# Loading the last two kept weight units into dead query and key buffers, and making mean and eps of the group norms on VectorE

## The chip, the cores and the metric

One Trainium2 chip; the kernel runs on one of its cores. The metric is the device time of one execution in microseconds (us), the median of the runs shown. Engines are named as in the profile: PE is TensorE (matmuls and transposes; PEld its weight loads), DVE is VectorE, ACT is ScalarE, POOL is GpSimd, SP is SyncE, which here only issues transfers. A "q" behind an engine's name means its queue of instructions.

## The reference

Two layers of an encoder on 256 tokens of width 1024, in float32. Each layer has a mixer and a channel part:

```python
def mixer_sublayer(x, n1, w_in_l, qg, kg, rpb_l, og, w_out_l, tables):
    h = rms_norm(x, n1)
    proj = h @ w_in_l                                  # 1024 -> 2560
    qa, ka, va, qd, kd, vd, qc, kc, vc = jnp.split(proj, cuts, axis=-1)
    ...                                                # q and k: norm per head, rotary for d and c
    out_a = neighbourhood_attention(qa, ka, ...)       # 4 heads
    out_d = dilated_window_attention(qd, kd, ...)      # 6 heads
    out_c = gqa_block_attention(qc, kc, ...)           # 6 heads of queries, 2 of keys
    mix = jnp.concatenate([rms_norm(out_a, og[:NA_W]), rms_norm(out_d, ...), rms_norm(out_c, ...)], axis=-1)
    return x + mix @ w_out_l                           # 1024 -> 1024

def channel_sublayer(x, n2, w_gu, cw, cb, w_dn):
    g, u = jnp.split(rms_norm(x, n2) @ w_gu, 2, axis=-1)      # 1024 -> 2 x 2816
    g = depthwise_conv_centred(g, cw, cb)                     # 3 taps along the tokens
    return x + (jax.nn.gelu(g, approximate=False) * u) @ w_dn # 2816 -> 1024
```

The three norms of `mix`, one for each group of heads, are the group norms of the title: `lax.rsqrt(mean(x*x) + EPS)` over the 256 or 384 columns of a group.

## The kernel before, in words

**Weights.** Every float32 weight is split into a high part (rounded to the format that PE multiplies, by a cast on ACT) and a low part (the rest, by a subtraction on DVE), and a product is made of three matmuls: high by high, high by low, low by high (`mm3`). The weights come in units of up to 128 x 2048 numbers, in the order of use: 12 units of the input projection, 6 of the output projection, 33 of the channel part, for each layer. `unit()` hands out the next unit; it first issues loads up to four units ahead into a ring of four buffers (`raw`, queue of SP), and splits up to two units ahead into a ring of two pairs of buffers (`hi` and `lo` in the pool `wp`). A unit's pair comes free when its last matmul is done.

**Kept units.** The 6 units of the output projection of the second layer are split early, during the channel part of the first layer (`keep`), and their parts are stored in DRAM (`dram_khi`, `dram_klo`). When such a unit is due, `split` has nothing to split: it loads both parts with two transfers from the queue of POOL into the next pair of the ring. Units 0 to 3 of the six have 128 x 1536 numbers a part (768 KB), units 4 and 5 have 128 x 1024 (512 KB). In this document "unit 0" to "unit 5" are these six.

**Mixer.** PE weaves the matmuls of the projections between the small ones of the attention (scores, transposes of the probabilities, weighing of the values). Queries and keys of one kind of head lie in tiles `act_q..` and `act_k..` as high and low part: `qo`, `ko` for the dilated and the neighbourhood heads, `qc`, `kc` for the grouped heads. The last scores that read `qc` and `kc` are those of heads 10 and 11; the neighbourhood heads come after them. `mixed` writes each pair of heads' output into `mixT` as high and low part and adds up the squares on POOL (`act_sqm`). `group_rstd` turns the squares with PE (two transposes), sums them on DVE (`small_ss`) and calls `rstd_of`: mean and eps (`small_ms`), then the power -0.5 (`small_rstd`), both on POOL. `rstd_of` also serves the norms per head, there with `width` 64. The output projection of a group runs without the norm; DVE multiplies by it when it adds the product to `xs` (`const_x`): four such updates for each group, one for each half of the tokens and of the columns.

**From the mixer to the channel part.** Units 4 and 5 are the last group's: unit 4 the left half of the columns, unit 5 the right half. When the left half of `const_x` is up to date, PE transposes it (8 transposes), ACT and DVE write it as high and low part into `act_hT`, and the first matmuls of the channel part read that.

**Order.** The kernel records every operation (`Plan.add`), and a planner (`Plan.order`) then writes them out engine by engine: of all operations that could start it takes the one that it expects to start first, by its own costs for each kind of operation, and between equal ones that with the lower rank. The rank is the place in the program plus a shift (`later`) plus a number from the table `PLACES`, which holds one for some of the operations. Every engine runs its instructions in the written order. All of them are issued on one line, so every row of the profile names L472, and rows are told apart by their tiles.

Of the kernel before, what the change touches and what calls it, by code (L numbers as in the profile page):

```python
# [12 lines left out]
F32R = mybir.dt.float32r  # L13
I32 = mybir.dt.int32
AF = mybir.ActivationFunctionType
ALU = mybir.AluOpType
AX = mybir.AxisListType

P = 128
# [4 lines left out]
HD = 64  # L24
# [12 lines left out]
UNIT = 2048  # L37
# [187 lines left out]
def handover(a, b):  # L225
# [1 line left out]


PLACES = {
# [6 lines left out]
}  # L236


class Plan:
# [5 lines left out]
    def pool(self, real, name, bufs, space=bass.MemoryType.SB):  # L245
        return PlanPool(self, real, name, bufs, space)
# [271 lines left out]
def encoder_kernel(  # L518
# [21 lines left out]
    nc = Plan(tc)  # L540
# [5 lines left out]
    act = pool("act", 2)  # L546
# [19 lines left out]
    def load_x(c, n, by):  # L566
        cs = slice(c * P, (c + n) * P)
        by.dma_start(xs[:, :, cs], xv[:, :, cs])
# [53 lines left out]
    raws, parts, taken = [], [], [0]  # L622
# [3 lines left out]
    kept = {}  # L626
# [16 lines left out]

    def load(i):
        v = views[i]
        if i in kept:
            raws.append(None)
            return
        a, b = v.shape[1], v.shape[2]
        raw = wp.tile([P, UNIT], F32, tag="raw", name=f"raw{i}", bufs=RAWS)  # L650
        rv = raw[:, : a * b].rearrange("p (a b) -> p a b", b=b)
        if i == 0:
            for by, what, c in START:
                by = nc.scalar if by == "act" else nc.sync
                if what == "w":
                    by.dma_start(rv[:, c], v[:, c])
                elif what == "x":
                    load_x(*c, by)
                elif what == "ident":
                    by.dma_start(ident, c_ident)  # L660
                elif what == "g":
                    by.dma_start(gl0 if c == 0 else gl1[16 * c - 16 : 16 * c], gsrc[c])
            nc.first_loads = len(nc.ops)
        else:
            for c in range(0, a, 2 if i == 1 else a):
                e = c + 2 if i == 1 else a
                nc.sync.dma_start(rv[:, c:e], v[:, c:e])
        raws.append(raw)

    def split(i):  # L670
        v = views[i]
        a, b = v.shape[1], v.shape[2]
        n = a * b
        raw = raws[i]
        hi = wp.tile([P, UNIT], F32R, tag="hi", name=f"hi{i}", bufs=PARTS)
        lo = wp.tile([P, UNIT], F32R, tag="lo", name=f"lo{i}", bufs=PARTS)
        h = b if i < 2 else b * max(1, CHUNK // b)
        if i in kept:
            for d, z in zip(kept[i], (hi, lo)):
                nc.gpsimd.dma_start(z[:, :n], d)  # L680
        for c in range(0, n if i not in kept else 0, h):
            e = min(c + h, n)
            nc.scalar.copy(hi[:, c:e], raw[:, c:e])
            nc.vector.tensor_tensor(lo[:, c:e], raw[:, c:e], hi[:, c:e].bitcast(F32), op=ALU.subtract)
        r = lambda z: z[:, :n].rearrange("p (a b) -> p a b", b=b)
        parts.append((r(hi), r(lo)))

    def unit():

        i = taken[0]  # L690
        taken[0] += 1
        with nc.later(SPLIT_LATER):
            while len(raws) < min(i + AHEAD + RAWS - PARTS, len(views)):
                load(len(raws))
            while len(parts) < min(i + AHEAD, len(views)):
                split(len(parts))
        return parts[i]
# [6 lines left out]
    def rstd_of(ss, n, width, eps, name):  # L704

        ms = small.tile([P, n], F32, tag="ms", name=f"ms_{name}")
        nc.gpsimd.tensor_scalar(ms, ss, 1.0 / width, eps, ALU.mult, ALU.add)
        r = small.tile([P, n], F32, tag="rstd", name=f"rstd_{name}")
        nc.gpsimd.tensor_tensor(r, ms, minus_half[:, :n], op=ALU.pow)
        return r  # L710
# [161 lines left out]
    def tables_of(l):  # L872
        for which in "qk":
            tables["d" + which, l] = tables_d(l, which)
        for which in "qk":
            tables["c" + which, l] = tables_c(l, which)

    load(0)
    for l in range(DEPTH):

        hT = act.tile([P, KD, 2, S], F32R, tag="hT", name=f"hT{l}", bufs=1)
        hT_hi, hT_lo = hT[:, :, 0], hT[:, :, 1]
        if l == 0:
            gains_T(0, 1)
            split(0)
# [656 lines left out]
```

## Time and profile before

| | |
|---|---|
| median of 3 runs | 611.07 us (609.97 to 611.33) |
| the profiled execution: its time, its span | 611.12 us, 609.3 us |
| granted TensorE clock, mean | 0.999 |
| PE busy | 600.6 us, 99% of the span |
| DVE busy | 484.9 us, 80% |
| ACT busy | 428.4 us, 70% |
| POOL busy | 84.6 us, 14% |
| moved by DMA | 121.44 MB, 199 GB/s over the span |
| instructions | 9892 |

The span runs from the first to the last instruction; the execution's time has 1.8 us more around it. Matmuls are pipelined: one that is shown with 0.39 us is followed by the next 0.23 us later, so a busy PE may still wait, and short waits are read from the distance of two starts rather than from the busy share. The layers follow each other as mixer (to about 121 us), channel part (to 305), mixer (to 420), channel part.

### The profile page before, as it was taken

The page shows a single profiled execution, that of the slowest core. Times are in us where ns is not written, and L with a number is a line of the kernel's source. Part 1 is how long each engine was busy: PE and PEld are TensorE (multiplying, and loading weights), DVE is VectorE, ACT ScalarE, POOL GpSimd, SP SyncE. Part 2 cuts the span into 40 slices and gives each one's busy share as a digit, 9 for nine tenths or more (in the row PEclk, how much of TensorE's full clock was granted, in tenths as well). Part 3 has the DMA queues.
Part 4 walks back from the last instruction along what each step waited for, and adds up shares of the span by engine and source line. Part 5 has one row for each costly group of instructions (what it writes and reads, how often), then busy time and mean ns, then how long its engine had stood idle before and what let it go on. Part 6 is the DMA issues. An engine that isn't in the chain of part 4 may idle for free.

```text
span 609.3 us, 9892 instructions
## 1 busy us (share of the span) xinstructions
PE 600.6 (99%) x3496; PEld 525.2 (86%) x3496; DVE 484.9 (80%) x989; ACT 428.4 (70%) x1065; POOL 84.6 (14%) x136
## 2 busy tenths in 40 slices
PE   8999999999999999999999999999999999999997
PEld 6999898888888888888899989887888888888886
DVE  4899987998779886978788898758977777777775
ACT  6889999686657666766598898757765556665661
POOL 2733130202400000000032214232000000000000
PEclk9999999999999999999999999999999999999999
DMA  8994223656598996999445626554666556556501
GB/s 272 296 294 143 62 79 107 208 175 240 185 219 288 318 338 220 373 311 305 142 142 189 224 70 242 184 199 139 208 207 200 169 185 208 173 176 204 198 10 69
DMA packets 85217, 121.44 MB, mean 199 GB/s; under 512 B 9880, under 2 KB 69880, under 8 KB 85168
## 3 DMA queue, kind: packets, MB, share of 16 engines
q1 hardware_dynamic: 82896, 112.17, 56.8%
q0 software_dynamic: 1728, 8.39, 4.0%
q8 instruction: 27, 0.44, 0.3%
q10 hardware_dynamic: 544, 0.26, 0.2%
q14 instruction: 22, 0.18, 0.1%
HBM read 110.93 MB, written 9.88 MB: 198 GB/s over the span
## 4 chain that ended last, share of the span: by engine, by line
PE 91%; POOL 2%; issue 2%; DMA 2%; ACT 1%; DVE 1%; SPq 0%; DVEq 0%; POOLq 0%
PE psw_w L472 50%; PE psa_a L472 41%; DMA wp_hi<-dram_khi 1%; POOL small_rstd L472 1%; DMA wp_raw<-in_w_in_dram 1%; ACT act_s2k L472 1%; POOL small_ms L472 0%; DVE const_x L472 0%; ACT act_hT L472 0%; POOL act_sck L472 0%; POOL act_scq L472 0%; ACT wp_hi L472 0%; SPq L472 0%; POOL const_gq L472 0%; POOL act_sqm L472 0%
## 5 line engine op out<-in xcount | busy, mean ns | idle before, releaser
L472 DVE TENSOR_TENSOR wp_lo<-wp_raw,wp_hi 128x512 fp32r<-128x512 f32 (+2 forms) x332 | 232.3, 734 | 55.1 <-ACT wp_hi L472 34.9
L472 ACT CAST wp_hi<-wp_raw 128x512 fp32r<-128x512 f32 (+2 forms) x332 | 202.4, 663 | 25.1 <-PE psw_w L472 9.9
L472 PE MATMUL psw_w<-act_hT,wp_hi 128*128 128x512 f32 x704 | 180.7, 393 | 0.0
L472 PEld LDWEIGHTS psw_w<-act_hT,wp_hi 128*128 128x128 f32 x704 | 127.8, 189 | 24.2
L472 PE MATMUL psa_a<-wp_hi,act_hT 128*128 128x384 f32 (+2 forms) x448 | 113.3, 333 | 2.0 <-ACT act_hT L472 1.3
L472 PEld LDWEIGHTS psw_w<-act_hT,wp_lo 128*128 128x128 f32 x704 | 98.4, 190 | 7.1
L472 PE MATMUL psw_w<-act_hT,wp_lo 128*128 128x256 f32 x704 | 103.0, 282 | 0.0
L472 PEld LDWEIGHTS psa_a<-wp_hi,act_hT 128*128 128x128 f32 x448 | 77.9, 189 | 5.0 <-ACT act_hT L472 1.6
L472 ACT COPY act_s2k<-psw_w 128x256 f32<-128x256 f32 x88 | 32.4, 373 | 61.7 <-PE psw_w L472 61.4
L472 PE MATMUL psa_a<-wp_lo,act_hT 128*128 128x384 f32 (+2 forms) x224 | 74.0, 332 | 0.1
L472 PE MATMUL psa_a<-wp_hi,act_cl 128*128 128x512 f32 (+1 forms) x176 | 68.8, 393 | 0.0
L472 PE MATMUL psa_a<-wp_lo,act_ch 128*128 128x512 f32 (+1 forms) x176 | 68.7, 392 | 0.0
L472 PE MATMUL psa_a<-wp_hi,act_ch 128*128 128x512 f32 (+1 forms) x176 | 68.3, 392 | 0.0
L472 DVE TENSOR_TENSOR act_s2k<-psw_w,act_s2k 128x256 f32<-128x256 f32 x88 | 36.6, 421 | 16.2 <-ACT act_s2k L472 15.9
L472 PEld LDWEIGHTS psa_a<-wp_lo,act_hT 128*128 128x128 f32 x224 | 42.2, 188 | 2.1 <-DVE wp_lo L472 1.0
L472 PEld LDWEIGHTS psa_a<-wp_hi,act_cl 128*128 128x128 f32 x176 | 33.1, 188 | 7.4
L472 PEld LDWEIGHTS psa_a<-wp_hi,act_ch 128*128 128x128 f32 x176 | 33.2, 189 | 6.7
L472 PEld LDWEIGHTS psa_a<-wp_lo,act_ch 128*128 128x128 f32 x176 | 33.1, 188 | 6.8
L472 DVE SCALAR_TENSOR_TENSOR act_s2k<-act_s2k,act_cw,act_s2k 128x255 f32<-128x255 f32 x88 | 36.8, 477 | 1.4 <-ACT act_s2k L472 1.3
L472 ACT ACTIVATE act_s2k<-act_s2k 128x512 f32<-128x512 f32 x22 | 13.9, 632 | 29.6 <-DVE act_s2k L472 29.6
L472 ACT ACTIVATE act_s2k<-act_s2k,act_cw 128x256 f32<-128x256 f32 x44 | 24.1, 595 | 15.0 <-DVE act_s2k L472 15.0
L472 POOL TENSOR_TENSOR small_rstd<-small_ms,const_mh 128x6 f32<-128x6 f32 (+2 forms) x26 | 31.3, 1204 | 2.1
(120 smaller groups left out, 795.2 us busy)
## 6 DMA issues: line engine op xcount, KB each, us to landing
wp_raw<-in_w_gate_up_dram SPq DMA_DIRECT2D x44, 1024.0 KB, 5.2
wp_raw<-in_w_down_dram SPq DMA_DIRECT2D x22, 1024.0 KB, 4.9
wp_raw<-in_w_in_dram SPq DMA_DIRECT2D x14, 768.0 KB, 4.7
wp_raw<-in_w_in_dram SPq DMA_DIRECT2D x8, 1024.0 KB, 8.9
wp_raw<-in_w_out_dram SPq DMA_DIRECT2D x8, 768.0 KB, 10.0
dram_khi<-act_mixT_hi SPq DMA_DIRECT2D x4, 768.0 KB, 4.4
dram_klo<-act_mixT_lo SPq DMA_DIRECT2D x4, 768.0 KB, 11.2
wp_lo<-dram_klo POOLq DMA_DIRECT2D x4, 768.0 KB, 4.7
```

What stands on the lines that cost most here:

```text
L472: getattr(o.engine.real, o.method)(*map(real, o.args), **{k: real(v) for k, v in o.kw.items()})
```

## The change

Three things are changed.

1. Units 4 and 5 of the kept ones (those whose two parts fit where one full unit would, `2 * n <= UNIT`) no longer go through the ring. Their four loads are issued by `load`, so up to two units earlier in the program, into the buffers of `kc` (unit 4) and `qc` (unit 5), which are dead once the scores of the grouped heads are done; the buffers grow from 768 to 1024 columns. `split` only passes the tiles on. The first channel units therefore follow units 2 and 3 in the ring.
2. `rstd_of` makes mean and eps on DVE where `width` is over 64, that is for the six group norms. The power stays on POOL.
3. `PLACES` has other numbers, so the planner writes another order.

```diff
 PLACES = {
-    539: 34, 543: 38, 665: 15, 834: 24, 881: 160, 919: 134, 926: 7, 974: -38, 1092: 342, 1180: -15, 1181: -15,
...
+    375: -35, 488: 15, 528: -53, 550: 173, 587: -78, 594: 125, 616: -286, 646: -9, 709: -79, 750: -226, 752: -396,
...
     def load(i):
         v = views[i]
+        a, b = v.shape[1], v.shape[2]
+        n = a * b
         if i in kept:
             raws.append(None)
+            if 2 * n <= UNIT:
+                zs = [act.tile([P, n], F32R, tag=f"{'qk'[i % 2]}c{j}", name=f"kept{i}{j}", bufs=1) for j in range(2)]
+                for z, d in zip(zs, kept[i]):
+                    nc.gpsimd.dma_start(z, d)
+                raws[-1] = [z.rearrange("p (a b) -> p a b", b=b) for z in zs]
             return
-        a, b = v.shape[1], v.shape[2]
...
     def split(i):
...
         raw = raws[i]
+        if isinstance(raw, list):
+            parts.append(raw)
+            return
...
     def rstd_of(ss, n, width, eps, name):

         ms = small.tile([P, n], F32, tag="ms", name=f"ms_{name}")
-        nc.gpsimd.tensor_scalar(ms, ss, 1.0 / width, eps, ALU.mult, ALU.add)
+        by = nc.vector if width > HD else nc.gpsimd
+        by.tensor_scalar(ms, ss, 1.0 / width, eps, ALU.mult, ALU.add)
```

POOL, second half of the mixer of layer 2, before. `dram_khi` and `dram_klo` are the kept parts, `wp_hi_240` with `wp_lo_248` is one pair of the ring and `wp_hi_141` with `wp_lo_149` the other; 1536 columns mark units 2 and 3 here, 1024 columns unit 4:

```order
L472 TENSOR_SCALAR small_ms_454<-small_ss_4031 128x2
L472 TENSOR_TENSOR small_rstd_460<-small_ms_454,const_mh_85 128x2
L472 DMA wp_lo_248<-dram_klo_2446 128x1536
L472 TENSOR_TENSOR act_sqm_866<-act_sqm_866,act_sqm_967 128x256
L472 DMA wp_hi_240<-dram_khi_2431 128x1536
L472 DMA wp_lo_149<-dram_klo_2618 128x1536
L472 DMA wp_hi_141<-dram_khi_2583 128x1536
L472 TENSOR_TENSOR act_sqm_866<-act_sqm_866,act_sqm_967 128x256
L472 TENSOR_SCALAR small_ms_300<-small_ss_1189 128x2
L472 TENSOR_TENSOR small_rstd_328<-small_ms_300,const_mh_85 128x2
L472 DMA wp_hi_240<-dram_khi_2730 128x1024
L472 DMA wp_lo_248<-dram_klo_2759 128x1024
```

The same place now, from the loads of unit 1:

```order
L472 DMA wp_lo_149<-dram_klo_2309 128x1536
L472 DMA wp_hi_141<-dram_khi_2281 128x1536
L472 DMA act_kc_965<-dram_klo_2742 128x1024
L472 TENSOR_TENSOR small_rstd_460<-small_ms_454,const_mh_85 128x2
L472 DMA act_kc_959<-dram_khi_2725 128x1024
L472 DMA act_qc_809<-dram_khi_2846 128x1024
L472 DMA act_qc_818<-dram_klo_2860 128x1024
L472 TENSOR_TENSOR act_sqm_881<-act_sqm_881,act_sqm_950 128x256
L472 DMA wp_hi_240<-dram_khi_2443 128x1536
L472 DMA wp_lo_248<-dram_klo_2478 128x1536
L472 DMA wp_lo_149<-dram_klo_2619 128x1536
L472 DMA wp_hi_141<-dram_khi_2589 128x1536
```

The four loads of units 4 and 5 moved from the end of the mixer to a place ahead of units 2 and 3, the first of them ahead of the first group's power. Of unit 2 the high part is now loaded first, with no addition of squares between its two loads; before it came second, behind such an addition. The rows of mean and eps (`small_ms`) are gone from this queue.

PE, end of the mixer of layer 2, before. `psa` are the sums of the output projection (unit 4 in 157 and 175, unit 5 in 302 and 332), the rows with `const_x` transpose its left half:

```order
L472 MATMUL psa_a_175<-wp_lo_248,act_mixT_hi_856 128x512
L472 MATMUL psa_a_175<-wp_hi_240,act_mixT_lo_916 128x512
L472 MATMUL psa_a_157<-wp_lo_248,act_mixT_hi_856 128x512
L472 MATMUL psa_a_157<-wp_hi_240,act_mixT_lo_916 128x512
L472 MATMUL psw_w_117<-const_ident_89,const_x_79 128x128 x4
L472 MATMUL psw_w_83<-const_ident_89,const_x_79 128x128 x4
L472 MATMUL psa_a_302<-wp_hi_141,act_mixT_hi_856 128x512
L472 MATMUL psa_a_302<-wp_lo_149,act_mixT_hi_856 128x512
L472 MATMUL psa_a_302<-wp_hi_141,act_mixT_lo_916 128x512
```

The same place now (unit 4 in 157 and 302, unit 5 in 332 and 175):

```order
L472 MATMUL psa_a_302<-act_kc_965,act_mixT_hi_875 128x512
L472 MATMUL psa_a_302<-act_kc_959,act_mixT_lo_920 128x512
L472 MATMUL psa_a_332<-act_qc_809,act_mixT_hi_875 128x512
L472 MATMUL psa_a_332<-act_qc_818,act_mixT_hi_875 128x512
L472 MATMUL psw_w_83<-const_ident_89,const_x_79 128x128
L472 MATMUL psw_w_117<-const_ident_89,const_x_79 128x128
L472 MATMUL psa_a_332<-act_qc_809,act_mixT_lo_920 128x512
L472 MATMUL psa_a_332<-act_qc_809,act_mixT_hi_875 128x512
L472 MATMUL psa_a_332<-act_qc_818,act_mixT_hi_875 128x512
L472 MATMUL psa_a_332<-act_qc_809,act_mixT_lo_920 128x512
L472 MATMUL psw_w_83<-const_ident_89,const_x_79 128x128 x3
L472 MATMUL psw_w_117<-const_ident_89,const_x_79 128x128 x3
```

Between the two transposes of the last group's squares and the first transpose of `const_x` stood 12 matmuls of 512 columns, all of unit 4; now 17 stand there, three of unit 3, the 12 of unit 4 and two of unit 5. Four more of unit 5 lie between the first two and the other six transposes, and six behind them, where all 12 were.

DVE at the same time, before. `small_ss` sums the squares of the last group, `small_rstd_351` is its power, `small_rstd_328` that of the second group; the rows with `const_x` are the updates, those with `wp_lo` split units of the channel part:

```order
L472 SCALAR_TENSOR_TENSOR const_x_79<-psa_a_302,small_rstd_328,const_x_79 128x512
L472 SCALAR_TENSOR_TENSOR const_x_79<-psa_a_332,small_rstd_328,const_x_79 128x512
L472 TENSOR_REDUCE small_ss_1418<-psw_w_124 128x2
L472 COPY act_cw_1498<-psw_w_166 128x88
L472 SCALAR_TENSOR_TENSOR const_x_79<-psa_a_175,small_rstd_351,const_x_79 128x512
L472 SCALAR_TENSOR_TENSOR const_x_79<-psa_a_157,small_rstd_351,const_x_79 128x512
L472 TENSOR_TENSOR wp_lo_248<-wp_raw_138,wp_hi_240 128x512 x3
```

And now:

```order
L472 TENSOR_REDUCE small_ss_1412<-psw_w_166 128x2
L472 COPY act_cw_1500<-psw_w_124 128x88
L472 TENSOR_SCALAR small_ms_344<-small_ss_1412 128x2
L472 SCALAR_TENSOR_TENSOR const_x_79<-psa_a_175,small_rstd_328,const_x_79 128x512
L472 TENSOR_TENSOR wp_lo_149<-wp_raw_95,wp_hi_141 128x512 x2
L472 SCALAR_TENSOR_TENSOR const_x_79<-psa_a_157,small_rstd_351,const_x_79 128x512
L472 TENSOR_TENSOR wp_lo_149<-wp_raw_95,wp_hi_141 128x512
L472 SCALAR_TENSOR_TENSOR const_x_79<-psa_a_302,small_rstd_351,const_x_79 128x512
```

An update of the second group went from ahead of the sum to behind it, mean and eps stand on DVE, and three splits went in between and ahead of the two updates that the transposes need.

10 rows, old and new, of the table PLACES are left out of this document.

## The prediction

> **What bounds the kernel now.** I read the page's busy times first, then the same by stage, then TensorE's timeline wherever the distance of two starts shows a wait.
>
> ```profile
> span 609.3 us, 9892 instructions
> PE 600.6 (99%) x3496; PEld 525.2 (86%) x3496; DVE 484.9 (80%) x989; ACT 428.4 (70%) x1065; POOL 84.6 (14%) x136
> 8.00:121.00 113.00, 112.12 (x747) 101.08 (x746) 100.20 (x252) 99.40 (x324) 36.35 (x55) 1.00 0.59 183
> 305.00:420.00 115.00, 113.57 (x757) 103.21 (x755) 90.84 (x239) 93.09 (x309) 31.37 (x47) 1.00 0.53 175
> 420.00:605.00 185.00, 185.00 (x990) 159.02 (x988) 139.83 (x237) 110.95 (x203) 1.26 (x3) 1.00 0.51 168
> ```
>
> A row by stage gives window, length, busy time of PE, PEld, DVE, ACT and POOL, clock, DMA share and GB/s. PE is busy 185.00 of 185 us in the last channel part, at clock 1.00, and the change takes no matmul away. So only waits of PE can be won: 0.88 us by these rows in the first mixer, 1.43 us in the second. Since pipelined matmuls cover part of a wait, the distances of starts tell more:
>
> ```profile
> 397.66 0.47 PE L472 MATMUL psa_a<-wp_hi,act_mixT_lo 128*128 128x512 f32 x1
> 398.39 0.50 PE L472 MATMUL psa_a<-wp_hi,act_mixT_hi 128*128 128x512 f32 x1 [0.26 <-DMA wp_hi<-dram_khi]
> ...
> 411.53 0.38 PE L472 MATMUL psw_w<-const_ident,act_sqm 128*128 128x128 f32 x2
> ...
> 414.18 0.40 PE L472 MATMUL psa_a<-wp_lo,act_mixT_hi 128*128 128x512 f32 x1
> 414.42 0.40 PE L472 MATMUL psa_a<-wp_hi,act_mixT_lo 128*128 128x512 f32 x1
> 415.92 1.09 PE L472 MATMUL psw_w<-const_ident,const_x 128*128 128x128 f32 x8 [1.10 <-DVE const_x L472]
> ```
>
> A 512-column matmul starts 0.24 us after the one before it (414.18 to 414.42). Against that pace PE loses 398.39 - 397.66 - 0.24 = 0.49 us on the high part of unit 2, and 415.92 - 414.42 - 0.24 = 1.26 us on `const_x` at the end of the mixer. These are the two waits that the change can reach best.
>
> **Unit 2's loads.** Before, POOL issues the low part, adds squares, then issues the high part:
>
> ```profile
> 390.19 0.60 POOL L472 DMA_DIRECT2D wp_lo<-dram_klo  x1 [5.12 <-PE psa_a L472]
> 390.81 0.75 POOL L472 TENSOR_TENSOR act_sqm<-act_sqm,act_sqm 128x256 f32<-128x256 f32 x1
> 391.50 0.57 POOL L472 DMA_DIRECT2D wp_hi<-dram_khi  x1
> wp_lo<-dram_klo POOLq DMA_DIRECT2D x1, 768.0 KB, 4.7
> wp_hi<-dram_khi POOLq DMA_DIRECT2D x1, 768.0 KB, 6.8
> ```
>
> The last two rows are the DMA view: KB and us from issue to landing. The pair lands at 390.19 + 4.7 = 394.9 and 391.50 + 6.8 = 398.3. The first matmul that needs the high part starts at 398.39, so the row's releaser is right. Now the high part goes first, from 390.2 when the buffers come free, and is there at about 394.9; the low part, wanted one matmul later, follows at about 390.8 + 6.8 = 397.6 at worst. Without the wait both are wanted at 397.9 to 398.2. The 0.49 goes; what is late next is the low part, by nothing or by 0.1.
>
> **The four early loads.** They need the end of the last scores that read `kc` and `qc`:
>
> ```profile
> 383.44 0.98 PE L472 MATMUL psw_w<-act_kc,act_qc 64*128 64x256 f32 x12
> 384.35 0.72 POOL L472 TENSOR_TENSOR small_rstd<-small_ms,const_mh 128x2 f32<-128x2 f32 x1
> 411.15 0.57 POOL L472 DMA_DIRECT2D wp_lo<-dram_klo  x1
> wp_lo<-dram_klo POOLq DMA_DIRECT2D x1, 512.0 KB, 4.0
> wp_hi<-dram_khi POOLq DMA_DIRECT2D x1, 512.0 KB, 4.7
> 371.55 0.37 SPq L472 DMA_DIRECT2D wp_raw<-in_w_down_dram  x1
> 395.84 0.32 SPq L472 DMA_DIRECT2D act_s2k<-in_conv_w_dram  x1
> L472 POOL DMA_DIRECT2D wp_hi<-dram_khi x6: 530/543/625, 371.0 to 411.7; - x6
> L472 POOL DMA_DIRECT2D wp_lo<-dram_klo x6: 530/586/787, 370.2 to 411.2; - x6
> ```
>
> The first can go at 383.44 + 0.98 = 384.4. The last two rows hold the least, median and longest issue: POOL is held 0.53 to 0.79 us by each. In the new queue the first load, the first group's power (0.72), three more loads and an addition (0.75) stand ahead of unit 2: with about 0.5 of gaps POOL gets there at 386.4 + 4h, h being the hold per load. With h = 0.55 that is 388.6, before unit 2's buffers come free at 390.2. The power comes 0.65 later; it is queued behind the first load, and DVE's updates of unit 0 wait for it, but unit 0's matmuls run until 390.2. I price that at nothing. As transfers, a pair of 512 KB lands 4.0 and 0.57 + 4.7 = 5.3 after the first issue, so 1.3 more per load, and four land at 384.4 + 4.0 + 3 x 1.3 = 392.3. SP issues nothing between 371.55 and 395.84, so they meet no other load. Unit 2's high part may be served behind them by under a microsecond (0 to 0.8 of the 3 it has from 394.9 to 397.9). Units 4 and 5 are wanted from about 412: 20 us early.
>
> **The end of the mixer.** Let T be the start of the squares' transposes (411.53). The chain to `const_x`:
>
> ```profile
> 412.82 0.41 DVE L472 TENSOR_REDUCE small_ss<-psw_w 128x2 f32<-128x256 f32 x1
> 414.45 1.41 DVE L472 SCALAR_TENSOR_TENSOR const_x<-psa_a,small_rstd,const_x 128x512 f32<-128x512 f32 x2 [1.06 <-PE psa_a L472]
> 413.33 0.19 POOL L472 TENSOR_SCALAR small_ms<-small_ss 128x2 f32<-128x2 f32 x1 [1.07 <-DVE small_ss L472]
> 413.61 0.71 POOL L472 TENSOR_TENSOR small_rstd<-small_ms,const_mh 128x2 f32<-128x2 f32 x1
> L472 DVE RECIPROCAL small_rs<-small_rs 128x2 f32<-128x2 f32 x32 | 5.1, 159 | 3.2 <-ACT act_s2k L472 3.0
> 115.22 1.28 DVE L472 TENSOR_TENSOR wp_lo<-wp_raw,wp_hi 128x512 fp32r<-128x512 f32 x2
> ```
>
> Before, the sum of squares started at T + 1.29 behind two updates, the power was done at 414.32 = T + 2.8, but the updates ran from T + 2.92, when unit 4's matmuls let them, and the transposes started at T + 4.39. PE had nothing to put between: unit 5's loads were issued with unit 4's, at 411.15 and later, and landed by 411.72 + 4.7 = 416.4.
>
> Now the sum starts near T + 0.3 and is done at T + 0.7; mean and eps on DVE are not shown by this trace, and the nearest row is the reciprocal of the same shape, 0.16 us. Behind a copy that gives T + 1.1, and the power T + 1.9. DVE's queue meanwhile has one update (0.7, from about T + 1.2 when unit 3's three matmuls are through), two splits (1.28), the first update of unit 4 (0.7), a split (0.64) and the second update. The first is done at T + 4.0, the second at T + 5.4. PE has 17 matmuls, so reaches the first transposes at T + 0.25 + 17 x 0.24 = T + 4.3, and, two transposes (0.2) and four matmuls later, the other six at T + 5.5. Both waits end before PE comes; margin 0.3 and 0.1, so I take 0.15 as left of the 1.26: gain 1.1. What is late next is `act_hT`: behind the last transpose 6 matmuls (1.4 us) cover ACT's and DVE's writing, where 12 (2.9 us) did. I keep 0 to 0.8 of loss for that in the range.
>
> **First mixer and tail.**
>
> ```profile
> 117.45 0.40 PE L472 MATMUL psa_a<-wp_hi,act_mixT_lo 128*128 128x512 f32 x1
> 117.90 0.44 PE L472 MATMUL psw_w<-const_ident,const_x 128*128 128x128 f32 x2
> 115.23 0.72 POOL L472 TENSOR_SCALAR small_ms<-small_ss 128x2 f32<-128x2 f32 x1 [2.83 <-DVE small_ss L472]
> 116.03 1.03 POOL L472 TENSOR_TENSOR small_rstd<-small_ms,const_mh 128x2 f32<-128x2 f32 x1
> 604.83 0.39 PE L472 MATMUL psa_a<-wp_hi,act_cl 128*128 128x512 f32 x1
> 605.03 0.48 DVE L472 SCALAR_TENSOR_TENSOR const_x<-psw_w,small_rx,const_x 128x256 f32<-128x256 f32 x1 [0.55 <-PE psw_w L472]
> 605.43 0.74 DVE L472 SCALAR_TENSOR_TENSOR const_x<-psa_a,small_rx,const_x 128x512 f32<-128x512 f32 x1
> ```
>
> In the first mixer mean and eps took 0.72 on POOL beside DVE's splits; on DVE, at 0.16, the chain is some 0.5 shorter, and PE's wait there, 117.90 - 117.45 - 0.24 = 0.21, mostly goes: gain 0.15, bounds 0 and 0.2. At the very end the last update starts 0.4 after the one ahead of it; in the new order that one's matmuls end some eight earlier, so the last follows its own matmul: gain 0.15, bounds 0 and 0.3. Six times mean and eps on DVE add 6 x 0.16 = 1 us to an engine at 80%, off the path elsewhere: nothing.
>
> **The sum.** 0.49 + 1.1 + 0.15 + 0.15 = 1.9, less 0.1 for the low part of unit 2. From the profiled execution's 611.12 (span 609.3 and 1.8 around it; 0.05 over the median, so no correction): 609.3 us. About 0.2%, 1.2 us, is what a measurement of this kernel can tell from no change.
>
> **Rivals.**
>
> *A. The new order brings waits of its own.* PE's order differs from before nearly from end to end. The old order has waits of 0.2 to 0.5 at places where DVE, ACT or a load comes late; four new ones of 0.4 take 1.6 of the 1.8: 610.9, no change. For it: margins of 0.1 to 0.3 above, and PE waits at few places now, so more places can get a wait than lose one. Against: the places that I followed gain. Chance 0.18. With over 3 us of such waits it would be 612.4 or more: 0.08.
>
> *B. POOL's queue holds unit 2 up (slower).* All loads share POOL's queue in order. Unit 2's high part lands 4.7 after its issue and is wanted at 396.7 to 397.9 (396.7 if PE comes there with nothing else to weave in), so PE is late once POOL arrives after 392.0: 386.4 + 4h > 392.0, h over 1.4. With 1.4 gained elsewhere, it is slower by over 1.2 once PE's wait passes 2.6: h over 2.05. If each load held POOL until it landed, 4.3 from the rows above, POOL would arrive at 403.6: a wait of 11.6, and 621. Against it: twelve issues at 0.53 to 0.79, though DVE was busy 90.84 of 115 us. Chance 0.10 in both forms, since this trace has no four loads in a row.
>
> The milder form is an issue that waits until DVE is between two pieces of work. A burst of DVE as quoted, two updates (1.41) alone or with two splits (1.28) behind them, gives h = 0.55 + 1.41 = 2.0 or 0.55 + 2.69 = 3.2, arrival at 394.4 or 399.2, a wait of PE of 2.4 or 7.2, and 611.12 - 1.4 + 2.4 = 612.1 or 616.9. I give this 0.06 and the hold until landing 0.04.
>
> The Trainium skill, "SBUF — State Buffer", says in the box on the "DVE blocks DMA" trap (section on the two sides of SBUF) that a load from GpSimd's queue cannot have its descriptors written while VectorE runs an operation that takes the port they share. It speaks against this change, which puts four such loads in a row beside VectorE's work; the twelve issues of this trace do not show such a hold.
>
> *C. The order removes more.* Other small waits may go too: the first mixer's row leaves 0.88 us idle, of which I counted 0.15. With the other 0.73 gone, and the 0.25 that I left standing: 609.3 - 1.0 = 608.3. Chance 0.04.
>
> *D. The loads are early in the program but not in time,* because they wait in order behind the last scores. The working above says 384.4 against 411.15; it would take 27 us to undo them. Under 0.02.
>
> **How the numbers follow.** The forecast holds 0.60, from 608.4 to 609.9 by the bounds of its terms; C adds 0.04 and D none. A's 0.18 lies between 609.9 and 612.3, nearly all within 1.2 of no change; A's tail (0.08) and B (0.10) are slower. So faster 0.64, same 0.17, slower 0.19. The range takes in the forecast, C and nearly all of A: 608.1 to 612.0, and leaves out B and A's tail, 0.18.
>
> **What would show it.** Right: four loads issued at 384 to 388 and landed by 393; unit 2's high part issued by 391; no `DMA wp_hi<-dram_khi` on PE; the sum of squares before T + 0.5, and under 0.3 lost at the first transposes of `const_x`; last update within 0.2 of its matmul. Wrong: loads that hold POOL over 1.4 us, PE waiting for `act_hT` at the start of the channel part, or distances over 0.35 at many other places.

## The result: 1.5 us faster

| | before | changed |
|---|---|---|
| median | 610.31 us (609.97 to 611.33, 9 runs) | 608.81 us (607.83 to 610.04, 9 runs) |
| the profiled execution: its time, its span | 611.12 us, 609.3 us | 608.41 us, 606.6 us |

The ratio is 0.9972, with a 95% interval of 0.9963 to 0.9981: 1.2 to 2.3 us less. The forecast was 609.3, 1.8 us below the first median of before (611.07, three runs); the difference measured over nine runs each is 1.5. The forecast time lies 0.5 above the measured one; the median of before itself fell by 0.8 with more runs. The two profiled executions lie 2.7 us apart, more than the medians do: that of before is 0.8 above its median, the changed one 0.4 below.

### The profile page after: what moved, and what is told of

The parts are those of the page before. It is cut to its first block, busy times and chain, and to the rows that moved or that the text cites. A ratio compares the mean times of both kernels' runs of the same rounds, so it can differ in the third digit from the quotient of the medians.

```text
span 606.6 us, 9899 instructions
## 1 busy us (share of the span) xinstructions
PE 600.9 (99%) x3496; PEld 526.7 (87%) x3496; DVE 484.9 (80%) x995; ACT 428.6 (71%) x1065; POOL 80.9 (13%) x130
## 4 chain that ended last, share of the span: by engine, by line
PE 96%; ACT 2%; DVE 1%; POOL 0%; issue 0%; DVEq 0%; ACTq 0%; POOLq 0%
PE psw_w L472 53%; PE psa_a L472 43%; ACT act_s2k L472 1%; ACT wp_hi L472 0%; DVE act_z L472 0%; DVE wp_lo L472 0%; POOL small_rstd L472 0%; ACT act_z L472 0%; ACT act_hT L472 0%; DVE act_sw L472 0%; POOL small_ms L472 0%; DVE const_x L472 0%; DVE act_qo L472 0%; POOL const_warm L472 0%; DVEq L472 0%
## 5 line engine op out<-in xcount | busy, mean ns | idle before, releaser
L472 DVE TENSOR_TENSOR wp_lo<-wp_raw,wp_hi 128x512 fp32r<-128x512 f32 (+2 forms) x332 | 231.5, 731 | 59.1 <-ACT wp_hi L472 39.3
L472 ACT CAST wp_hi<-wp_raw 128x512 fp32r<-128x512 f32 (+2 forms) x332 | 203.0, 663 | 22.8 <-PE psw_w L472 10.2
L472 PE MATMUL psw_w<-act_hT,wp_hi 128*128 128x512 f32 x704 | 180.4, 393 | 0.0
L472 PEld LDWEIGHTS psw_w<-act_hT,wp_hi 128*128 128x128 f32 x704 | 127.8, 189 | 24.8 <-DVE act_hT L472 0.7
L472 PE MATMUL psa_a<-wp_hi,act_hT 128*128 128x384 f32 (+2 forms) x448 | 113.1, 333 | 0.7 <-ACT wp_hi L472 0.7
L472 PEld LDWEIGHTS psw_w<-act_hT,wp_lo 128*128 128x128 f32 x704 | 97.7, 190 | 6.8
L472 PE MATMUL psw_w<-act_hT,wp_lo 128*128 128x256 f32 x704 | 102.2, 282 | 0.0
L472 PEld LDWEIGHTS psa_a<-wp_hi,act_hT 128*128 128x128 f32 x448 | 78.3, 189 | 3.4 <-ACT wp_hi L472 0.9
L472 ACT COPY act_s2k<-psw_w 128x256 f32<-128x256 f32 x88 | 32.4, 373 | 62.2 <-PE psw_w L472 61.9
L472 PE MATMUL psa_a<-wp_lo,act_hT 128*128 128x384 f32 (+2 forms) x224 | 74.4, 334 | 0.1
L472 PE MATMUL psa_a<-wp_lo,act_ch 128*128 128x512 f32 (+1 forms) x176 | 68.9, 392 | 0.0
L472 PE MATMUL psa_a<-wp_hi,act_ch 128*128 128x512 f32 x176 | 68.8, 392 | 0.0
L472 PE MATMUL psa_a<-wp_hi,act_cl 128*128 128x512 f32 (+1 forms) x176 | 68.5, 393 | 0.0
L472 DVE TENSOR_TENSOR act_s2k<-psw_w,act_s2k 128x256 f32<-128x256 f32 x88 | 36.6, 421 | 14.5 <-ACT act_s2k L472 14.1
L472 PEld LDWEIGHTS psa_a<-wp_lo,act_hT 128*128 128x128 f32 x224 | 42.2, 189 | 2.4 <-DVE wp_lo L472 1.0
L472 PEld LDWEIGHTS psa_a<-wp_hi,act_cl 128*128 128x128 f32 x176 | 33.1, 188 | 7.5
L472 PEld LDWEIGHTS psa_a<-wp_hi,act_ch 128*128 128x128 f32 x176 | 33.2, 189 | 6.7
L472 PEld LDWEIGHTS psa_a<-wp_lo,act_ch 128*128 128x128 f32 x176 | 33.1, 188 | 6.7
L472 DVE SCALAR_TENSOR_TENSOR act_s2k<-act_s2k,act_cw,act_s2k 128x255 f32<-128x255 f32 x88 | 36.7, 477 | 1.4 <-ACT act_s2k L472 1.3
L472 ACT ACTIVATE act_s2k<-act_s2k 128x512 f32<-128x512 f32 x22 | 13.9, 631 | 30.2 <-DVE act_s2k L472 30.2
L472 ACT ACTIVATE act_s2k<-act_s2k,act_cw 128x256 f32<-128x256 f32 x44 | 24.1, 595 | 15.3 <-DVE act_s2k L472 15.3
L472 POOL TENSOR_TENSOR small_rstd<-small_ms,const_mh 128x6 f32<-128x6 f32 (+2 forms) x26 | 30.8, 1186 | 14.4 <-DVE small_ms L472 12.8
```

What stands on the lines that cost most here:

```text
L472: getattr(o.engine.real, o.method)(*map(real, o.args), **{k: real(v) for k, v in o.kw.items()})
```

## The profile after

The page's span and the second mixer's row by stage, which before held 113.57 us of PE in 115:

```profile
span 606.6 us, 9899 instructions
305.00:420.00 115.00, 115.00 (x773) 105.43 (x772) 93.00 (x243) 95.26 (x315) 31.46 (x47) 1.00 0.57 192
```

PE's timeline of before, at three landmarks (first wide matmul, first matmul of the channel part in either layer):

```profile
7.50 0.44 PE L472 MATMUL psa_a<-wp_hi,act_hT 128*128 128x384 f32 x1 [1.30 <-ACT act_hT L472]
120.94 0.40 PE L472 MATMUL psw_w<-act_hT,wp_hi 128*128 128x512 f32 x1
419.65 0.40 PE L472 MATMUL psw_w<-act_hT,wp_hi 128*128 128x512 f32 x1
```

The changed kernel at the same landmarks, at unit 2 (396.44, 398.11), at the end of the second mixer, and its last matmul:

```profile
7.30 0.44 PE L472 MATMUL psa_a<-wp_hi,act_hT 128*128 128x384 f32 x1
120.14 0.50 PE L472 MATMUL psw_w<-act_hT,wp_hi 128*128 128x512 f32 x1
396.44 0.63 PE L472 MATMUL psa_a<-wp_hi,act_mixT_hi 128*128 128x512 f32 x2
398.11 0.47 PE L472 MATMUL psa_a<-wp_lo,act_mixT_hi 128*128 128x512 f32 x1
409.64 0.38 PE L472 MATMUL psw_w<-const_ident,act_sqm 128*128 128x128 f32 x2
413.90 0.38 PE L472 MATMUL psw_w<-const_ident,const_x 128*128 128x128 f32 x2
415.05 0.81 PE L472 MATMUL psw_w<-const_ident,const_x 128*128 128x128 f32 x6
417.09 0.40 PE L472 MATMUL psw_w<-act_hT,wp_hi 128*128 128x512 f32 x1
602.32 0.39 PE L472 MATMUL psa_a<-wp_hi,act_cl 128*128 128x512 f32 x1
```

From one channel part's first matmul to the other's, before took 419.65 - 120.94 = 298.71 us and the changed kernel 417.09 - 120.14 = 296.95: 1.76 less, which is the two waits, 0.49 and 1.26. The first mixer, from the first wide matmul, took 113.44 and 112.84: 0.6 less. That number is soft: in the profiles of the experiments below, kernels with before's order took 114.39 and 113.53 there, and five more with the changed order 112.86 to 113.75. From the second channel part's first matmul to the last one it is 185.2 in both (604.83 - 419.65 and 602.32 - 417.09). What lies behind the last matmul's start fell from 4.48 to 4.32.

POOL's timeline, the landings (KB, us from issue), one row by windows (its last two numbers are the DMA share, where 1 is all 16 transfer engines busy, and GB/s), and two rows of DVE:

```profile
384.05 0.53 POOL L472 DMA_DIRECT2D act_kc<-dram_klo  x1 [3.47 <-PE psw_w L472]
385.28 0.57 POOL L472 DMA_DIRECT2D act_kc<-dram_khi  x1
386.37 0.55 POOL L472 DMA_DIRECT2D act_qc<-dram_klo  x1
390.40 0.57 POOL L472 DMA_DIRECT2D wp_hi<-dram_khi  x1
390.97 0.55 POOL L472 DMA_DIRECT2D wp_lo<-dram_klo  x1
wp_hi<-dram_khi POOLq DMA_DIRECT2D x1, 768.0 KB, 5.6
wp_lo<-dram_klo POOLq DMA_DIRECT2D x1, 768.0 KB, 7.1
act_kc<-dram_khi POOLq DMA_DIRECT2D x1, 512.0 KB, 6.1
act_qc<-dram_klo POOLq DMA_DIRECT2D x1, 512.0 KB, 7.6
386.50:396.00 9.50, 9.50 (x69) 7.93 (x68) 6.65 (x24) 7.24 (x24) 2.21 (x4) 1.00 1.03 347
410.56 0.16 DVE L472 TENSOR_SCALAR small_ms<-small_ss 128x2 f32<-128x2 f32 x1
602.75 0.75 DVE L472 SCALAR_TENSOR_TENSOR const_x<-psa_a,small_rx,const_x 128x512 f32<-128x512 f32 x1 [1.35 <-PE psa_a L472]
```

POOL is held 0.53 to 0.57 us by each of these loads, no longer than before (0.53 to 0.79). But the four early loads end at 386.37 + 7.6 = 394.0, and unit 2's parts land at 396.0 and 398.1: the low part in the very moment in which the row at 398.11 wants it. From 386.5 to 396.0 the transfer engines are full (DMA share 1.03), so unit 2's loads, issued at 390.4 and 391.0, move only as the ones ahead of them are through. Mean and eps take 0.16 us on DVE, and the last update (602.75) starts as its matmul ends (602.32 + 0.39).

## The experiments

Theory M is the prediction's: each term sits at its place. Theory O says that the new numbers of `PLACES` brought the gain and the rest came along. The change has three parts, and a table's numbers belong to operations, so they can be carried over to the other kernel's operations. All ratios are to before run beside the kernel.

| loads of units 4, 5 | mean, eps | PLACES | us, ratio with interval |
|---|---|---|---|
| ring | POOL | old | before |
| early | POOL | old | 611.17, 1.0012 (1.0004 to 1.0021) |
| early | DVE | old | 611.03, 1.0008 (1.0000 to 1.0017) |
| ring | POOL | new | 618.43, 1.0120 (1.0103 to 1.0136) |
| ring | DVE | new | 610.51, 1.0001 (0.9992 to 1.0009) |
| early | POOL, but in the order planned for DVE | new | 610.44, 0.9998 (0.9987 to 1.0008) |
| early | DVE | new | the change: 608.81, 0.9972 (0.9963 to 0.9981) |

The planner writes a new order for each of them except the last but one, so two rows differ by more than the part that is named. Mean and eps on DVE with the ring and the old numbers was not run.

**The loads alone.** The edit is the change's own, with the second part undone and the old numbers put back:

```diff
 PLACES = {
+    ...                        # the old numbers, at the operations' new positions
...
-        by.tensor_scalar(ms, ss, 1.0 / width, eps, ALU.mult, ALU.add)
+        nc.gpsimd.tensor_scalar(ms, ss, 1.0 / width, eps, ALU.mult, ALU.add)
```

> The kernel before with the first part of the change alone: the early loads of units 4 and 5, the old numbers of PLACES (carried over to the operations' new positions), mean and eps on POOL. Theory M (each term at its place; the loads let unit 5's matmuls fill the end of the second mixer): the 1.27 us wait for const_x goes, since 19 instead of 12 matmuls stand ahead of the transposes; unit 2's high part still comes behind its low part and an addition, so that wait of 0.5 stays or grows by some tenths behind four more loads. 1.0 to 1.3 us faster than before, 609.0 to 609.3. Rival O (the gain comes from the new order of PLACES, the loads are only carried along): within 0.4 of before, 610.3.

It came out slower, by 0.2 to 1.3 us. PE's timeline of this kernel, at the transposes of `const_x` and at the start of the channel part:

```profile
416.04 0.39 PE L472 MATMUL psa_a<-act_qc,act_mixT_hi 128*128 128x512 f32 x1
416.76 1.09 PE L472 MATMUL psw_w<-const_ident,const_x 128*128 128x128 f32 x8 [0.33 <-DVE const_x L472]
418.61 0.39 PE L472 MATMUL psa_a<-act_qc,act_mixT_lo 128*128 128x512 f32 x1
419.01 0.50 PE L472 MATMUL psw_w<-act_hT,wp_hi 128*128 128x512 f32 x1
419.70 0.28 PE L472 MATMUL psw_w<-act_hT,wp_lo 128*128 128x256 f32 x1
420.12 0.50 PE L472 MATMUL psw_w<-act_hT,wp_hi 128*128 128x512 f32 x1
```

The wait for `const_x` fell from 1.26 to 416.76 - 416.04 - 0.24 = 0.48, as M said in kind. But the old order puts all eight transposes together and leaves five matmuls behind them, and PE then waits for `act_hT`: 0.16 at 419.01, 0.30 at 420.12 (a 256-column matmul is followed 0.12 later), more after it. From the second channel part's first matmul (419.01) to the last one (605.10) it is 186.1 us instead of 185.2: 0.9 lost, more than the 0.8 that the wait for `const_x` gave. The gain is handed on to the next wait in line. Theory M's time, 609.0 to 609.3, fell, and O's too, since this is slower than before.

**The loads back in the ring.** The change without its first part, with the new numbers carried over:

```diff
-            if 2 * n <= UNIT:
-                zs = [act.tile([P, n], F32R, tag=f"{'qk'[i % 2]}c{j}", name=f"kept{i}{j}", bufs=1) for j in range(2)]
...
-                raws[-1] = [z.rearrange("p (a b) -> p a b", b=b) for z in zs]
```

> The changed kernel without its first part: units 4 and 5 go through the ring again, everything else as changed (new numbers of PLACES, mean and eps on DVE). Theory M: the end of the second mixer loses again, 1 us or so at the transposes of const_x and up to 1.4 us at unit 5, whose loads can only start when unit 3's buffers come free: 1.0 to 2.4 us slower than the changed kernel, 609.8 to 611.2. Rival O: within 0.4 of the changed kernel, 608.8.

```profile
413.83 0.40 PE L472 MATMUL psa_a<-wp_hi,act_mixT_lo 128*128 128x512 f32 x1
414.06 0.38 PE L472 MATMUL psw_w<-const_ident,const_x 128*128 128x128 f32 x2
415.07 0.87 PE L472 MATMUL psw_w<-const_ident,const_x 128*128 128x128 f32 x6 [0.62 <-DVE const_x L472]
417.07 0.50 PE L472 MATMUL psa_a<-wp_hi,act_mixT_hi 128*128 128x512 f32 x1 [1.12 <-DMA wp_hi<-dram_khi]
```

Two transposes go at 414.06 without a wait, the other six 0.8 us late (two take 0.22), and unit 5's first matmul 1.37 late (six take 0.63): its high part has only been issued at 412.08. The gain is gone, 610.51, inside M's 609.8 to 611.2. O falls: without the loads the new order is worth nothing.

**The new numbers alone,** and **both parts with the old numbers:**

```diff
 PLACES = {
+    ...                        # the other kernel's numbers, at this kernel's positions
```

> The kernel before with the new numbers of PLACES alone. Theory M: little, since the order cannot fill PE at the end of the mixer while the loads of units 4 and 5 wait for ring buffers; the smaller waits in the first mixer (0.2 to 0.4 us together) may go: 0 to 0.7 us faster than before, 609.6 to 610.4. Rival O: most of the measured gain of 1.5, so 609.0 or less.

> The first and second part of the change with the old numbers of PLACES. Theory M: the 1.27 us at the end of the second mixer go and up to 0.2 in the first one, unit 2's wait stays: 1.0 to 1.5 us faster than before, 608.8 to 609.3. Rival O: within 0.4 of before.

The new numbers on the old code cost 8 us, which neither theory had. PE's timeline at the end of the first mixer, and the same time by windows (length, busy time of PE, PEld, DVE, ACT, POOL, clock, DMA share, GB/s):

```profile
122.00 0.44 PE L472 MATMUL psw_w<-const_ident,const_x 128*128 128x128 f32 x2 [0.17 <-DVE const_x L472]
123.34 0.87 PE L472 MATMUL psw_w<-const_ident,const_x 128*128 128x128 f32 x6 [0.90 <-DVE const_x L472]
125.59 0.80 PE L472 MATMUL psw_w<-act_hT,wp_hi 128*128 128x512 f32 x1 [1.38 <-DVE act_hT L472]
122.00:125.60 3.60, 1.32 (x9) 0.84 (x9) 3.60 (x7) 3.56 (x9) 0.00 (x0) 0.89 0.00 0
125.60:128.00 2.40, 2.40 (x9) 2.21 (x10) 2.40 (x6) 2.40 (x7) 0.00 (x0) 0.50 0.00 0
128.00:130.00 2.00, 2.00 (x9) 1.72 (x9) 2.00 (x4) 2.00 (x8) 0.96 (x1) 0.50 0.39 109
130.00:132.00 2.00, 2.00 (x9) 1.75 (x8) 1.89 (x5) 0.43 (x2) 1.26 (x3) 0.60 1.06 366
```

With mean and eps on POOL the planner makes another order from these numbers, in which three waits follow each other in the first mixer. PE works 1.32 of 3.6 us there, and its clock is granted at 0.50 afterwards, until about 131.6. By the channel part's first matmul 4.7 us are lost (125.59 instead of 120.94); the rest of the 8 is lost behind it, the time at half clock among it. A table of this kind belongs to the code for which it was made.

Both parts with the old numbers came to 611.03 instead of M's 608.8 to 609.3. The wait for `const_x` is gone there (the transposes follow at the usual distance), but as with the loads alone 0.9 us is lost in the second channel part (186.1 instead of 185.2), and the first one begins at 121.39 instead of 120.94. So neither theory holds as it was put: the gain needs the loads and the new order together.

**Unit 2's high part first,** in the kernel before, nothing else moved. Operation 4036 is the load of the high part, 4037 that of the low part:

```diff
-            for i in self.order():
+            order = self.order()
+            a, b = order.index(4037), order.index(4036)
+            assert a < b
+            order.remove(4036)
+            order.insert(a, 4036)
+            for i in order:
```

> The kernel before, every instruction in its old place but one: on POOL, unit 2's high part is loaded ahead of its low part and of the addition of squares. Theory M (each wait has its own price and can be taken away alone): PE's distance at unit 2's first high part falls from 0.73 to 0.24 to 0.35 us, the low part may then be late by up to 0.1; 0.3 to 0.5 us faster than before, 610.0 to 610.2. Rival W (the wait only moves to unit 2's low part, which now comes behind): distance at the next matmuls up by 0.4, time as before, 610.5.

610.03 us against 610.54, ratio 0.9995 (0.9985 to 1.0004): by time alone unclear, but the trace shows it (the edit moves the line from L472 to L477):

```profile
396.92 0.48 PE L477 MATMUL psa_a<-wp_hi,act_mixT_lo 128*128 128x512 f32 x1
397.23 0.39 PE L477 MATMUL psa_a<-wp_hi,act_mixT_hi 128*128 128x512 f32 x1
wp_hi<-dram_khi POOLq DMA_DIRECT2D x1, 768.0 KB, 4.5
wp_lo<-dram_klo POOLq DMA_DIRECT2D x1, 768.0 KB, 5.9
```

The distance at unit 2 is 0.31 instead of 0.73. Both parts are in time, and the wait does not move on to the low part: W falls. From one channel part to the other this kernel takes 298.13 us, 0.58 less than before.

**Mean and eps back on POOL,** every instruction of the changed kernel in its place:

```diff
-                getattr(o.engine.real, o.method)(*map(real, o.args), **{k: real(v) for k, v in o.kw.items()})
+                getattr(self.moved.get(i, o.engine).real, o.method)(*map(real, o.args), **{k: real(v) for k, v in o.kw.items()})
...
+        if width > HD:
+            nc.moved[len(nc.ops) - 1] = nc.gpsimd   # planned as VectorE's, written out for GpSimd
```

> The changed kernel with every instruction in its place, except that mean and eps of the six group norms run on POOL, at the same place in the order. Theory M: at the end of the first mixer POOL is slow beside VectorE's splits, the power comes 0.7 to 0.9 later, and the transposes of const_x, which want both updates, wait 0.5 to 0.8 us; at the end of the second mixer the 0.3 us of margin hide it. 609.3 to 609.7. Rival Z (the prediction's 0.15 was the whole worth of that part, and the plan around it matters more): 608.7 to 609.0.

```profile
115.35 0.72 POOL L472 TENSOR_SCALAR small_ms<-small_ss 128x2 f32<-128x2 f32 x1 [1.92 <-DVE small_ss L472]
118.26 0.27 PE L472 MATMUL psw_w<-const_ident,const_x 128*128 128x128 f32 x1
118.69 0.98 PE L472 MATMUL psw_w<-const_ident,const_x 128*128 128x128 f32 x7 [0.16 <-DVE const_x L472]
```

In the first mixer PE now waits 0.32 at the second transpose (0.43 after the first, 0.11 being its pace). The first matmul of the channel part comes at 120.94, 0.5 after the 512-column matmul ahead of it, so 0.26 late where the changed kernel is 0.1 late: together 0.5, the lower end of M's wait. The median, 610.44 (608.42 to 611.63), is 1.0 to 1.6 above the changed kernel's two medians (608.81 and, below, 609.40), more than this and above the times of both theories. In its trace PE also waits at unit 2, 0.3 us for the high and 0.4 for the low part, which leads to the next question.

**What spreads the times.** Two kernels ran beside the last two above: the changed one with the four loads issued behind those of units 2 and 3, and the changed one with the four loads issued by SP. Then four more ran together: the changed kernel again, the four loads behind unit 3's again, all loads of kept units by SP, and before again. The edit for the loads behind unit 3's (4062 and 4063 are that unit's loads), and that for all loads by SP, of which the kernel with the four by SP has only the part in `load`:

```diff
+            early = (4037, 4036, 4060, 4061)         # the loads of units 4 and 5
+            order = [i for i in order if i not in early]
+            at = max(order.index(4062), order.index(4063)) + 1   # behind unit 3's
+            order[at:at] = early
```

```diff
-                nc.gpsimd.dma_start(z[:, :n], d)
+                nc.gpsimd.dma_start(z[:, :n].bitcast(F32), d)
+                nc.moved[len(nc.ops) - 1] = nc.sync  # written out for SP; likewise in load
```

> The changed kernel with every instruction in its place, except that POOL issues the four loads of units 4 and 5 behind the loads of units 2 and 3, 13 us later. Theory M (what counts is that they need no ring buffer, not that they come 25 us early): they land by 406, before unit 4 is wanted at 410.7, and unit 2's parts land 1 us earlier than in the changed kernel (4.7 and 6 us from issue instead of 5.6 and 7.1), where the low part has only 0.1 us to spare: 608.5 to 608.9, no change. Rival E (they must be early, or they meet the loads that follow): over 609.3, with a wait at unit 4.

> The changed kernel once more, beside the next three, for a second profile. Theory V (its executions differ because a load from POOL's queue sometimes lands 1.0 to 2.5 us late, and unit 2's low part has only 0.1 us to spare): times spread over about 2 us again, median 608.5 to 609.3; the second profile shows other loads late, and waits at unit 2 of 0 to 0.7 us. Rival (its executions are alike, the spread of 607.8 to 610.0 came from other stages): the same distances on PE at 396 to 399 us, and a spread that is no smaller where the loads come later.

> The changed kernel with the four loads behind those of units 2 and 3, once more and beside the changed kernel itself. Theory V: unit 2's parts have 1 us more to spare, so the median is 0.3 to 0.8 us below the changed kernel's, 608.1 to 608.5, and the spread under 1.2 us. Rival: within 0.2 of the changed kernel, spread as there.

> The changed kernel with every instruction in its place, except that SP issues the loads of all six kept units, so that none goes through POOL's queue. Theory D (the late landings are those of POOL's queue, whose loads VectorE's work holds up): no wait at unit 2, median 608.0 to 608.4, spread under 1 us. Rival N (they come from the memory or the transfer engines, whichever queue issues): median and spread as the changed kernel, 608.5 to 609.3 and 2 us.

> The changed kernel with every instruction in its place, except that SP instead of POOL issues the four loads of units 4 and 5. Theory M (POOL is held only for the issue, 0.53 to 0.57 us each): time within 0.3 of the changed kernel, the four land within 4 to 8 us as from POOL. Rival B (VectorE's work keeps POOL's loads from starting): they land over 1 us sooner from their issue than from POOL, and unit 2's parts too.

> The kernel before once more, for a second profile. Theory V: unit 2's high part landed 1.5 us late in the first profile (6.8 us from issue; 394.9 plus 1.9 for the transfer itself would have been 396.8, in time for 397.9), so the wait of 0.49 us is not in every execution: likely a distance of 0.24 to 0.4 us there now; the 1.26 us at the end of the second mixer are there again. Rival: both waits as before, since both follow from the order.

| kernel | median, us | from, to (executions) | ratio to before |
|---|---|---|---|
| changed, again | 609.40 | 608.14, 610.53 (11) | 0.9976 (0.9966 to 0.9985) |
| four loads behind unit 3's | 608.31 | 607.91, 608.82 (6) | 0.9966 (0.9953 to 0.9978) |
| the same, again | 608.33 | 608.02, 608.65 (5) | 0.9964 (0.9951 to 0.9978) |
| all kept loads by SP | 607.98 | 607.38, 608.20 (5) | 0.9955 (0.9943 to 0.9968) |
| the four loads by SP | 609.45 | 608.26, 611.21 (10) | 0.9985 (0.9974 to 0.9996) |

The second profile of the changed kernel is of an execution of 610.53 us, 2.1 longer than the first. PE's timeline and the landings:

```profile
398.14 0.28 PE L472 MATMUL psw_w<-act_ch,const_v 128*128 128x256 f32 x1
400.18 0.50 PE L472 MATMUL psa_a<-wp_lo,act_mixT_hi 128*128 128x512 f32 x1 [1.77 <-DMA wp_lo<-dram_klo]
wp_hi<-dram_khi POOLq DMA_DIRECT2D x1, 768.0 KB, 6.0
wp_lo<-dram_klo POOLq DMA_DIRECT2D x1, 768.0 KB, 9.1
```

Unit 2's low part took 9.1 us instead of 7.1, and PE waited 400.18 - 398.14 - 0.12 = 1.9 for it: nearly the whole difference of the two executions. Theory V had waits of 0 to 0.7 there, so it named the place and undersized the wait. The engines are full here too from 386.5 to 396.0 (share 1.03), so what is late seems to be a small rest. It can be seen at unit 3, whose loads also land 2.1 us later than in the first profile: in the row of 403.0 to 404.75 the DMA share is 0.06, about one of the 16 engines, where the first profile has 0.00.

```profile
403.00:404.75 1.75, 1.75 (x16) 1.63 (x14) 1.14 (x3) 1.07 (x2) 0.71 (x1) 1.00 0.06 25
```

With the four loads behind unit 3's:

```profile
398.21 0.28 PE L477 MATMUL psw_w<-act_ch,const_v 128*128 128x256 f32 x1
398.33 0.40 PE L477 MATMUL psa_a<-wp_lo,act_mixT_hi 128*128 128x512 f32 x1
wp_hi<-dram_khi POOLq DMA_DIRECT2D x1, 768.0 KB, 4.6
wp_lo<-dram_klo POOLq DMA_DIRECT2D x1, 768.0 KB, 6.2
391.21 0.54 POOL L477 DMA_DIRECT2D wp_lo<-dram_klo  x1
```

The low part comes 0.9 us ahead of its matmul (391.21 + 6.2 = 397.4), and PE does not wait. The engines have nothing to move from 386.5 to 390.0 (share 0.00), so unit 2's loads find nothing ahead of them. The spread falls from 2.4 to under 1; since fewer executions spread less, count them: all 11 of these two kernels are at 608.82 or below, but only 10 of the changed kernel's 20, the result's and these. The last of the four, issued at 399.48, lands 9.2 us later, at 408.7, still before unit 4 is wanted (410.7 in the changed kernel). So being early is worth nothing to them; needing no ring buffer is. Rival E fell, and V's median and spread came as expected. With all kept loads by SP, PE does not wait either, and this kernel has the lowest median of the study, 2.7 us below before (2.0 to 3.5), though its interval overlaps that of the four loads behind unit 3's. That is the time and spread of theory D; N fell.

With only the four by SP the times spread as in the changed kernel, though POOL no longer issues them; the spread goes when unit 2's loads are by SP too. That points to unit 2's own loads, but no slow execution of this kernel was profiled. In its profile (608.42 us) unit 2's parts land 4.4 and 6.7 us after their issue, 1.2 and 0.4 sooner than in the first profile of the changed kernel, and PE does not wait; where the four themselves landed, the profile does not show for SP's queue. The Trainium skill, "SBUF — State Buffer", box on the "DVE blocks DMA" trap, says that a load from GpSimd's queue has to wait for its descriptors while VectorE runs an operation that locks the port they share, and advises the queue of ScalarE or SyncE instead. The kernel with all kept loads by SP agrees with the advice, the one with four of them shows no gain from it; that VectorE's work is the cause, no run here shows. Why a rest of a load from POOL's queue comes late stays open: in the kernel with four loads behind, none of unit 2's was late in two profiles.

Before again gave 611.05 us, with the same two waits, 0.55 and 1.27: the theory that the first of them was chance fell. In both profiles of before the high part came 3.4 to 3.5 us after the low one where POOL added squares between the two loads, and 2.0 us apart in the kernel that issues them in one go.

## Why the prediction was right, point by point

- **The end of the second mixer.** Forecast: first transposes at T + 4.3, the others at T + 5.5, so the first channel matmul, six transposes and six matmuls later, at T + 7.5, with 0.15 left over. Measured, with T = 409.64: 4.26, 5.41 and 7.45, nothing left. DVE's chain ran as forecast too: the power done at T + 1.9, the two updates at T + 3.8 and T + 5.1. Right, and borne out by taking the loads back into the ring, which brought 0.8 and 1.4 back, though in an order that the planner wrote anew. That `act_hT` could be late next, with 0 to 0.8, did not come in the changed kernel. It came in the two kernels with early loads and the old order, where it took 0.9, and there I had not reckoned with it.
- **Unit 2's wait.** The 0.49 goes, as the edit to before showed. The mis-sized term is what replaced it. I had the four loads land by 392.3, the high part at 394.9, unit 2 behind the four "by under a microsecond" out of 3 to spare, and the low part at 397.6 at worst, with 0.1 lost. The four were through only at 394.0: I counted 1.3 us per load as if they were issued in one go, but POOL's power stands between the first two, and the second landed 3.0 us after the first (388.4 and 391.4). Nor is it so that they meet no other load: unit 1's high part, issued at 380.0 from the same queue, landed at 386.0. With the engines full, unit 2's parts landed 2.0 and 4.1 us behind the four, at 396.0 and 398.1: the high part 1.1 later than I had it, the low part without any margin, and in another execution at 400.1. PE also came to the high part at 396.44, not at 397.9, so 0.4 us was left of the 3. Against the kernel with the four loads behind, the changed kernel's median is 0.5 us (608.81 against 608.31, not side by side) to 1.1 us (side by side) higher; the intervals of the ratios overlap.
- **POOL's queue (rival B).** POOL was held 0.53 to 0.57 per load, so neither of its forms came. But there is a third form that I left out: the issue is short and the landing late. The row of 6.8 us in the profile before had that in it.
- **First mixer.** Forecast 0.15, measured 0.6 between landmarks in one pair of profiles; mean and eps on DVE are worth 0.5 of it in the new order, by the trace of the kernel that undoes them in place. That operation takes 0.16, as taken from the reciprocal's row.
- **Tail.** Forecast 0.15, measured 4.48 - 4.32 = 0.16.
- **The sum.** 1.8 forecast; 1.5 and 1.3 measured as differences of the medians in the two sets, 1.7 and 1.5 by their ratios, and 2.7 in the first profiles. That the sum came so close is in part luck. Two errors nearly cancelled: the first mixer gave some 0.4 more than I had, and unit 2's low part took as much or more back in the median. And the base of 611.12 was 0.4 to 0.8 above the later medians of before.
- **Rival A (new waits of the new order)** did not come in this kernel; with the same numbers on other code it came with 8 us.

## What to carry to other kernels

Freeing a load from the ring paid here only with an order that used it to put other work into the wait: neither the loads nor the order alone gained anything. Look at once for what is late next, and order that too. When a load is moved ahead of others in its queue, the margin of those behind it is what counts: issue it behind the ones that are wanted sooner, even if its own buffer is free. An order tuned for one version of the code was worth nothing here, or cost 8 us, on another.

## What the runs showed of the hardware

- A load of 768 KB from POOL's queue landed 4.4 to 9.1 us after its issue, while the issue itself held POOL 0.5 to 0.8 us. Loads issued in one go landed 1.2 to 1.4 us (512 KB) or 1.8 to 2.3 us (768 KB) apart in most pairs, and up to 3.7 us in the late ones.
- Loads of one queue that find the transfer engines full (DMA share 1.03 over 9.5 us) land behind all that was issued ahead of them: unit 2's high part 5.6 us after its issue behind the four, 4.5 to 4.6 without them.
- A PE that worked 1.32 of 3.6 us had its clock granted at 0.50 from there to 130 us and at 0.60 in the next two: short waits in a row cost more than their sum. In the same run it worked 2.67 of the 4 us from 422 to 426, and the clock stayed at 1.00. The Trainium skill, "TensorE: Matmul & The Clock Gate", part 1, tells of half rate after low activity; the trace agrees.
- Operations of 128x2 on POOL took longer when they began beside DVE's splits: mean and eps 0.56 to 0.72 us against 0.19, the power 1.03 to 1.08 against 0.71. Beside DVE's updates of `const_x` the power kept its 0.71.
